# A rotary step on packed rows: transfers collect the rotary rows of five tiles, VectorE turns them in two groups, transfers write them back

## The chip, the cores and the metric

The kernel runs on one core of a Trainium2 chip. The metric is the device time of one execution in microseconds (us). A TensorE, VectorE (DVE), ScalarE (ACT) and GpSimd (POOL) each work through their own list of instructions in order and wait for each other by semaphores; SyncE (SP) only issues transfers (DMAs), also in order. SBUF is the memory on the core with 128 partitions (rows of a tile), PSUM the one that TensorE writes to.

## The reference

One layer of a hybrid decoder, with 1024 tokens of width 1024 in float32. What matters here is the attention half of the token mixer and what stands around it:

```python
h = rmsnorm(x, pre_w_mix[l]) * (1.0 + sc1) + sh1
proj = h @ w_in[l]
aq, ak, av, hq, hf, hi, hg = jnp.split(proj, _SPLITS, axis=-1)
aq = partial_rope(aq.reshape(B, T, ATT_Q_HEADS, ATT_HEAD_DIM))     # 8 heads of 64
ak = partial_rope(ak.reshape(B, T, ATT_KV_HEADS, ATT_HEAD_DIM))    # 2 heads of 64
attn = sliding_window_sink_attention(aq, ak, av, attn_sinks[l])    # window 128
...
def partial_rope(x):                # the first 16 of the 64 numbers of a head
    x1, x2, rest = x[..., :8], x[..., 8:16], x[..., 16:]
    return jnp.concatenate([x1 * cos - x2 * sin, x2 * cos + x1 * sin, rest], axis=-1)
```

So only 16 of the 64 numbers of each head are turned by the rotary step; the other 48 pass. Behind it stand a gated linear recurrence (HGRN2), an output projection and a squared-ReLU MLP, which the change does not touch.

## The kernel before

Matrices are held as a high and a low part, and a product is three matmuls (high by high, high by low, low by high). Tokens are worked on in two halves of 512. The projection is made transposed: a tile `qT{th}_{u}` or `kT{th}` has 128 partitions, which are the 64 numbers of two heads, and 512 columns, which are the tokens of half `th`. There are four q tiles, one k tile and one v tile in each half.

The program is written as one list per engine. A small class `Queue` (lines 26 to 42, its call on line 39 is the line that almost all rows of the profile show) can pin an engine to the order in which the program is written; where an engine is not pinned, a scheduler orders its instructions when the program is built. `DVE.last = marks[...]` puts a piece of VectorE work right behind a marked instruction.

The stretch around the change has these steps.

1. The first half's q, k and v tiles are finished on TensorE. ScalarE copies each from PSUM (`evac`), while TensorE makes k and v of the second half (`pk`, `pv`) and then the second half's q tiles one after the other (`pq`, `q_later`). These q matmuls, and after them the `pv` matmuls with the weights `whv`, are filler: `feed(us)` puts so many of them between the steps of attention.
2. `rope` turns a tile: a VectorE shuffle exchanges rows 0 to 7 with 8 to 15 in each group of 32 partitions, POOL multiplies the shuffled copy by a sine table, VectorE multiplies the tile by a cosine table, and VectorE adds the two. All four run over the full 128 x 512 tile; the tables hold 1 and 0 where nothing is turned. Five tiles of the first half are turned in one go (line 728), before the first scores; the five of the second half one at a time (`rope_late`), between pieces of attention.
3. `attention(tb)` handles a block of 128 tokens in stages: scores `sc` on TensorE (two groups of four heads, `mp` 0 and 1), masked copy to `comb` (VectorE `COPY_PREDICATED`, ScalarE for the block before), maximum `mx` and shifts `nm`, `sd` on VectorE, eight exponentials with sums on ScalarE, `den`, `rd` and the product `comb` on VectorE and POOL, transposes `pT` on TensorE, masked copies `pc` and `pp` on VectorE, values `oT` on TensorE, squares `sqa`, their sum `sqr`, its transpose `ssp`, `ssc`, the root `r_att` on POOL, `dg` on VectorE, the broadcast `rb` on TensorE and the scaling of `aT` on VectorE. The blocks overlap: while block t is between its stages, t+1 and t+2 are in theirs.
4. `split_hv` loads the eight weights `whv` into a pool of three raw buffers (`raw_`), ScalarE copies the high part and VectorE takes the low part; the load into a buffer waits until the low part of the weight three before has been made. `mod_sums` puts one step of a weighted sum over `wada` tiles (`macc`, VectorE) into the stream.

The order on VectorE in step 3 is the program's: an instruction that waits there holds all that stand behind it. The same holds for SP's list of transfers.

Of the kernel before, what the change touches and what calls it, by code (L numbers as in the profile page):

```python
# [47 lines left out]
def hybrid_layer(ctx: ExitStack, tc: tile.TileContext, I, out, dbg=None):  # L48
# [807 lines left out]
    hgw = cload("hgw", [P, 1], pool=tiny1)  # L856
    DVE.last = marks["sqr"]
    lsum = tiny1.tile([P, 4], F32, tag="lsum", bufs=1, name="lsum")
    DVE.tensor_tensor(lsum, le[:, 0, :], le[:, 1, :], ALU.add)
    lrc = tiny1.tile([P, 4], F32, tag="lrc", bufs=1, name="lrc")  # L860
    DVE.reciprocal(lrc, lsum)
    lp = small.tile([P, 2, 4], F32, tag="lp", bufs=1, name="lp")
    DVE.tensor_tensor(lp, le, lrc.unsqueeze(1).broadcast_to([P, 2, 4]), ALU.mult)
    lcs = small.tile([P, 4], F32, tag="lcs", bufs=1, name="lcs")
    DVE.tensor_tensor(lcs, lp[:, 0, :], lp[:, 1, :], ALU.add)
    DVE.last = None
    lb = tiny1.tile([P, 4], F32, tag="lb", name="lb")
    DVE.tensor_tensor(lb, lcs, lp[:, 0, :], ALU.subtract)
    omlb = tiny1.tile([P, 4], F32, tag="omlb", name="omlb")
    DVE.tensor_scalar(omlb, lb, -1.0, 1.0, ALU.mult, ALU.add)  # L870

# [1047 lines left out]
```

## Time and profile before

| | |
|---|---|
| median of 3 runs | 1091.78 us (1091.12 to 1093.92) |
| the profiled execution | 1092.65 us, span 1090.8 us, mean TensorE clock 0.993 |
| TensorE matmul busy in the span | 1068.2 us, 98% |
| VectorE, ScalarE, POOL busy | 818.8, 585.4 and 373.9 us |
| data moved | 206.62 MB |

The busy time of TensorE is that of pipelined matmuls, so 98% says that it is seldom idle, not that it runs at its peak. An idle time of an engine costs something only where the end hangs on it. "Releaser" names the instruction whose semaphore ended a wait.

### The profile page before, as it was taken

Reading aid. Unit: us, or ns where it says so; the run is one execution under the profiler, and the core shown is the slowest. Engines: PE = TensorE matmul, PEld = TensorE weight load, DVE = VectorE, ACT = ScalarE, POOL = GpSimd, SP = SyncE. Lnnn points to the kernel's source line nnn. Section 1 sums busy time; section 2 is a strip of 40 time slices with the busy share of each in tenths; the row PEclk is TensorE's granted clock in tenths of the full one; section 3 lists DMA queues with packets and bytes.
Section 4 is the critical chain, followed back from the end, with each engine's and each line's share of the span. In section 5 each row is a group of like instructions: output and inputs, shape, how many; then the busy total and the mean of one; then the engine's idle time right before and its main releaser. Section 6 shows DMA issues by size and latency. Waiting matters only on the chain.

```text
span 1090.8 us, 15818 instructions
## 1 busy us (share of the span) xinstructions
PE 1068.2 (98%) x5339; PEld 867.1 (79%) x5339; DVE 818.8 (75%) x1345; ACT 585.4 (54%) x1205; POOL 373.9 (34%) x459
## 2 busy tenths in 40 slices
PE   8988999999999999999999999999999999999996
PEld 6766677788888888888888888888888888888885
DVE  4888988878866574559776758776778787899786
ACT  4544544364664764566655555555665544456435
POOL 1253211143234753432543444444333333300014
PEclk9998999999999999999999999999999999999998
DMA  9901300634310252324577776766998888998538
GB/s 355 364 14 43 123 11 1 224 118 134 117 59 28 89 187 93 133 82 144 193 242 250 255 255 224 254 236 238 319 354 305 268 290 273 308 310 276 172 97 139
DMA packets 103264, 206.62 MB, mean 189 GB/s; under 512 B 13200, under 2 KB 13712, under 8 KB 103184
## 3 DMA queue, kind: packets, MB, share of 16 engines
q1 hardware_dynamic: 87696, 158.06, 42.4%
q0 software_dynamic: 15200, 47.20, 14.1%
q8 instruction: 42, 0.69, 0.3%
q10 hardware_dynamic: 288, 0.36, 0.1%
q14 instruction: 38, 0.31, 0.1%
HBM read 150.52 MB, written 55.05 MB: 188 GB/s over the span
## 4 chain that ended last, share of the span: by engine, by line
PE 83%; DVE 7%; ACT 2%; POOL 1%; issue 1%; DVEq 0%; ACTq 0%; POOLq 0%
PE pda L39 16%; PE pua L39 14%; PE pdc L39 8%; PE po L39 8%; PE puc L39 7%; PE phg L39 4%; PE pu L39 4%; PE phq L39 4%; PE pdb L39 4%; PE phf L39 4%; PE pub L39 3%; PE o L39 1%; ACT comb L39 1%; PE pq L39 1%; DVE mx L39 1%; DVE comb L39 1%
## 5 line engine op out<-in xcount | busy, mean ns | idle before, releaser
L39 POOL TENSOR_TENSOR b<-b,b 128x512 f32<-128x512 f32 x64 | 88.1, 1376 | 218.6 <-DMA b<-w_dn 218.2
L39 ACT ACTIVATE dw<-dwr 128x512 fp32r<-128x512 f32 x72 | 45.4, 630 | 50.3 <-DMA dwr<-td 29.0
L39 ACT ACTIVATE s<-s 128x512 f32<-128x512 f32 x84 | 52.9, 631 | 32.2 <-DVE s L39 30.8
L39 DVE TENSOR_TENSOR acc<-pda,acc 128x512 f32<-128x512 f32 x68 | 46.6, 686 | 15.4 <-PE pda L39 14.8
L39 DVE TENSOR_TENSOR dw<-dwr,dw 128x512 fp32r<-128x512 f32 x72 | 51.7, 718 | 8.4 <-ACT dw L39 8.4
L39 POOL DMA_DIRECT2D td<-b x64 | 36.3, 567 | 19.0 <-POOL b L39 19.0
L39 POOL TENSOR_TENSOR rrf<-ssf,mhalf 128x1 f32<-128x1 f32 x7 | 7.7, 1107 | 101.8 <-DVE ssf L39 101.8
L39 ACT ACTIVATE s<-pua 128x512 f32<-128x512 f32 x28 | 16.7, 598 | 43.6 <-PE pua L39 43.3
L39 ACT ACTIVATE comb<-comb,nm 128x128 f32<-128x128 f32 x64 | 24.8, 388 | 26.5 <-DVE sd L39 21.8
L39 DVE TENSOR_TENSOR wt<-s,wt 128x512 fp32r<-128x512 f32 x42 | 35.9, 855 | 2.5 <-ACT wt L39 2.4
L39 ACT ACT_TABLE_LOAD x28 | 35.9, 1283 | 1.7 <-PEq L1912 1.2
L39 DVE SCALAR_TENSOR_TENSOR macc<-wada,cs,macc 128x512 f32<-128x512 f32 x42 | 34.1, 812 | 2.5 <-DMA wada<-wada 1.7
L39 POOL DMA_DIRECT2D b<-w_dn x64 | 34.4, 540 | 2.7 <-issue 2.7
L39 DVE TENSOR_TENSOR wt<-a,wt 128x512 fp32r<-128x512 f32 x42 | 33.9, 806 | 0.9 <-ACT wt L39 0.9
L39 PE MATMUL pua<-bt_0h,wt 128*128 128x512 f32 x84 | 32.7, 389 | 0.0
L39 PE MATMUL pua<-bt_1h,wt 128*128 128x512 f32 x84 | 32.7, 389 | 0.0
L39 PE MATMUL pua<-bt_2h,wt 128*128 128x512 f32 x84 | 32.7, 389 | 0.0
L39 PE MATMUL pua<-bt_3h,wt 128*128 128x512 f32 x84 | 32.7, 389 | 0.0
L39 DVE TENSOR_TENSOR s<-puc,s 128x512 f32<-128x512 f32 x14 | 9.7, 690 | 27.6 <-issue 26.2
L39 DVE TENSOR_TENSOR acc<-pdc,acc 128x512 f32<-128x512 f32 x36 | 24.6, 684 | 7.4 <-PE pdc L39 7.3
L39 PE MATMUL pdc<-dw,du_3h 128*128 128x512 f32 x96 | 29.6, 389 | 0.0
L39 PE MATMUL pda<-dw,du_7h 128*128 128x512 f32 x96 | 29.6, 389 | 0.0
(811 smaller groups left out, 3723.0 us busy)
## 6 DMA issues: line engine op xcount, KB each, us to landing
dur<-ud SPq DMA_DIRECT2D x112, 256.0 KB, 4.5
wada<-wada SPq DMA_DIRECT2D x64, 256.0 KB, 3.6
b<-w_dn POOLq DMA_DIRECT2D x64, 256.0 KB, 5.0
td<-b POOLq DMA_DIRECT2D x64, 256.0 KB, 3.4
dwr<-td SPq DMA_DIRECT2D x64, 256.0 KB, 4.1
a<-w_u SPq DMA_DIRECT2D x56, 256.0 KB, 4.3
dwr<-w_dn SPq DMA_DIRECT2D x48, 256.0 KB, 4.9
ud<-s SPq DMA_DIRECT2D x42, 256.0 KB, 3.3
```

Of the source, the lines that this page charges most:

```text
L39: ins = op(*args, **kw)
```

## The change

The input weights are laid out so that, in each q and k tile, the 16 turned numbers of the upper head are partitions 48 to 63 and those of the lower head partitions 64 to 79, with the two numbers of each pair beside each other. The rotary rows of a tile are then one block of 32 partitions, and the partner of a row is its neighbour.

- `gather` issues three transfers on SP for a tile: its 32 rows into a strip of `R`, and twice 16 rows (every second one) into the strip of `Rr`, so that `Rr` has the rows with neighbours exchanged. A strip starts at partition 0, 32 or 64.
- `rotate` is three VectorE operations for a group: `R` by cosine, `Rr` by sine, and the sum. The groups have 96 partitions (two q tiles and k) and 64 partitions (two q tiles).
- `scatter` writes the strips back into the tiles with one transfer each.

Shuffles and POOL's products are gone. The first half's k tile is copied from PSUM before q tiles 2 and 3, and v last; the transposes of v move one step later. In the second half the group with k waits for q tiles 0 and 1 and stands behind `sd` of block 1, the other one behind `pp` of block 1. The weights `whv` 0 to 2 are loaded by calls ahead of the gathers, the following ones when a buffer is used; SP is pinned to the written order until the last scatter. Six small operations on the decay bounds (`lsum` to `omlb`) move from the end of attention to the place behind the first rotation, the load of `hgw` moves forward, and the `macc` steps are divided: in blocks 2 to 5 one stands behind `sqr` and one behind the scaling of `aT`, where both stood behind `sqr`, and they start one block earlier.

```diff
-    swap = [(i + 8) % 16 if i < 16 else i for i in range(32)]
-
-    def rope(x, th):
-        sh = t_("rope")
-        DVE.stream_shuffle(sh, x, swap)
-        POOL.tensor_tensor(sh, sh, sinT[th], ALU.mult)
-        DVE.tensor_tensor(x, x, cosT[th], ALU.mult)
-        yield
-        DVE.tensor_tensor(x, x, sh, ALU.add)
-        yield
+    def gather(t, R, Rr, j):
+        SP.dma_start(R[32 * j:32 * j + 32, :], t[48:80, :])
+        for b in range(2):
+            SP.dma_start(Rr[32 * j + b:32 * j + 32:2, :], t[49 - b:80:2, :])
+
+    def rotate(R, Rr, n, th):
+        for t, tab in ((R, cosT), (Rr, sinT)):
+            DVE.tensor_tensor(t[:n, :], t[:n, :], tab[th][:n, :], ALU.mult)
+        DVE.tensor_tensor(R[:n, :], R[:n, :], Rr[:n, :], ALU.add)
+
+    def scatter(t, R, j):
+        SP.dma_start(t[48:80, :], R[32 * j:32 * j + 32, :])
...
         spread(tb - 1)
+        if 3 <= tb <= 6:
+            mod_sums(1, "rb")
         yield
...
+    for kb in range(3):
+        load_hv(kb)
+    pin(True, SP)
+    rr = [w_(f"rr{i}", (P, 2, 512)) for i in range(2)]
+    rr = [(t[:, 0], t[:, 1]) for t in rr]
...
         if kb < 6:
-            u = (0, 1, 5, 4, 2, 3)[kb]
-            evac(0, u, pu[u])
+            u = (0, 1, 4, 2, 3, 5)[kb]
+            t = evac(0, u, pu[u])
+            if kb < 5:
+                gather(t, *rr[kb // 3], kb % 3)
...
-    ropes = [rope(x, 0) for x in [ks[0]] + qs[0]]
-    for a, b in zip([None] + ropes, ropes + [None]):
-        if b:
-            next(b)
-        if a:
-            next(a)
+    rotate(*rr[0], 96, 0)
+    rotate(*rr[1], 64, 0)
+    for i, t in enumerate((qs[0][0], qs[0][1], ks[0])):
+        scatter(t, rr[0][0], i)
+    for i in range(2):
+        scatter(qs[0][2 + i], rr[1][0], i)
+    r1 = [m_(f"r1{i}") for i in range(4)]
+    gather(ks[1], r1[0], r1[1], 2)
     pin(False, ACT, DVE, POOL)
...
-    def rope_late(mark):
+    def rope_late(mark, i):
         old, DVE.last = DVE.last, marks[mark]
-        for _ in rope(late.pop(0), 1):
-            pass
+        rotate(r1[2 * i], r1[2 * i + 1], 64 if i else 96, 1)
         DVE.last = old
...
         def done():
-            late.append(evac(1, u, pst()))
+            gather(evac(1, u, pst()), *r1[2 * (u // 2):2 * (u // 2) + 2], u % 2)
...
-    rope_late("sd")
-    rope_late("sd")
     feed(4.0)
     step(1)
     step(1)
-    rope_late("sd")
+    rope_late("sd", 0)
+    scatter_late(0)
...
+        if t == 1:
+            mod_sums(1)
         if 1 < t < 6:
-            mod_sums(2, "sqr")
+            mod_sums(1, "sqr")
...
-        if t < 2:
-            rope_late("pp")
         if t == 0:
+            rope_late("pp", 1)
             split_hv(range(5, 6))
+            scatter_late(1)
+            pin(False, SP)
```

How VectorE's list stands at the first rotation, from the decay bound's `le` on. Before, the first seven of 15 rotary rows:

```order
L39 TENSOR_TENSOR le<-c_lbt,lmx 128x8
L39 STREAM_SHUFFLE rope<-kT_855 128x512
L39 TENSOR_TENSOR kT_855<-kT_855,rope_0_739 128x512
L39 STREAM_SHUFFLE rope<-qT_0_809 128x512
L39 TENSOR_TENSOR qT_0_809<-qT_0_809,rope_0_739 128x512
L39 TENSOR_TENSOR kT_855<-kT_855,rope 128x512
L39 STREAM_SHUFFLE rope<-qT_1_825 128x512
L39 TENSOR_TENSOR qT_1_825<-qT_1_825,rope_0_739 128x512
```

and now, all of it (`rr_816` is the group of two q tiles and k, `rr_817` that of two q tiles):

```order
L39 TENSOR_TENSOR le<-c_lbt,lmx 128x8
L39 TENSOR_TENSOR rr_816<-rr_816,rope_0_741 96x512
L39 TENSOR_TENSOR rr_816<-rr_816,rope_0_745 96x512
L39 TENSOR_TENSOR rr_816<-rr_816 96x512
L39 TENSOR_TENSOR rr_817<-rr_817,rope_0_741 64x512
L39 TENSOR_TENSOR rr_817<-rr_817,rope_0_745 64x512
L39 TENSOR_TENSOR rr_817<-rr_817 64x512
L39 TENSOR_TENSOR lsum<-le 128x4
```

Fifteen operations of 128 partitions became six of 96 or 64, and the six small ones on the decay bounds stand behind them.

SP's list at the same place, which had nothing between the loads `whv2r` and `whv3r` but the load of `hgw`. Here are the first strips, and the end of the first scatter with what stands behind it:

```order
L39 DMA whv2r<-w_hv 128x512
L39 DMA rr_816<-qT_0_819 32x512
L39 DMA rr_816<-qT_0_819 16x512 x2
L39 DMA rr_816<-qT_1_838 32x512
L39 DMA rr_816<-qT_1_838 16x512 x2
L39 DMA rr_816<-kT_856 32x512
L39 DMA rr_816<-kT_856 16x512 x2
L39 DMA rr_817<-qT_2_874 32x512
```

```order
L39 DMA kT_856<-rr_816 32x512
L39 DMA qT_2_874<-rr_817 32x512
L39 DMA qT_3_892<-rr_817 32x512
L39 DMA r_963<-kT_945 32x512
L39 DMA r_964<-kT_945 16x512 x2
L39 DMA r_963<-qT_0_1027 32x512
L39 DMA r_964<-qT_0_1027 16x512 x2
L39 DMA r_963<-qT_1_1090 32x512
L39 DMA r_964<-qT_1_1090 16x512 x2
L39 DMA qT_0_1027<-r_963 32x512
L39 DMA qT_1_1090<-r_963 32x512
L39 DMA kT_945<-r_963 32x512
```

Right behind these stands `whv3r<-w_hv`: the loads of the later weights are now queued behind the write-back of the second half's first group (`r_963`).

VectorE's list behind `sd` of block 1, where the group with the second half's k stands now (before: one shuffle, one product and one sum of `qT_1` at the same places, and six rotary operations on `kT` and `qT_0` behind `sd` of block 0, which are gone):

```order
L39 TENSOR_TENSOR sd_1138<-c_sinks,mx_1134 128x8
L39 TENSOR_TENSOR r_963<-r_963,rope_1_743 96x512
L39 TENSOR_TENSOR r_964<-r_964,rope_1_747 96x512
L39 TENSOR_TENSOR pc_1172<-pT_0_1173,c_fle 128x512
L39 TENSOR_TENSOR r_963<-r_963,r_964 96x512
L39 TENSOR_TENSOR pc_1172<-pT_1_1179,c_fle 128x512
L39 TENSOR_TENSOR den_1151<-sm_1142,es_1140 128x8
```

Two rotary operations stand ahead of the first `pc` and one between the two, where it was one and one. A little further on, the sum `ssc` and the factor `dg` stand later than they did: `ssc` behind two of the masked copies of block 2, and `dg` behind the low part of `whv5`.

```order
L39 TENSOR_TENSOR whv4l<-whv4r,whv4h 128x512
L39 COPY_PREDICATED comb_1257<-c_mle,sc_0_0_1258 128x256
L39 COPY_PREDICATED comb_1257<-c_mle,sc_0_1_1259 128x256
L39 TENSOR_REDUCE ssc_1274<-ssp_1272 128x1
L39 TENSOR_TENSOR whv5l<-whv5r,whv5h 128x512
L39 TENSOR_SCALAR dg_1280<-c_tab,r_att_1278 128x128
```

Before, `ssc` stood ahead of `whv4l`, and `whv5l` behind `dg`.

More of the change, by code (lines that the diff above doesn't have):

```diff
@@ L259, in load_split @@
         hi, lo = mk(name + "h", dt=F32R), mk(name + "l", dt=F32R)
-        for c in range(0, src.shape[1], 512):
+        for c in range(0, 512 if src is None else src.shape[1], 512):
             rw = load_raw(raw_, f"{name}r{c}", src[:, c:c + 512]) if raw is None else raw
@@ L514, in hybrid_layer @@
         if kb == 6:
+            hgw = cload("hgw", [P, 1], pool=tiny1)
             lbt = cload("lbt", [P, 2, 4], pool=tiny1)
@@ L705, in hybrid_layer, with load_hv @@
     att = [attention(tb) for tb in range(TB)]
+    hvr = []
+    def load_hv(kb):
+        hvr.append(load_raw(raw_, f"whv{kb}r", I["w_hv"][kb]))
+    for kb in range(3):
[3 more added lines that the diff above has]
+    rr = [(t[:, 0], t[:, 1]) for t in rr]
     pu1 = [a_ps("pk1")]
@@ L727, in hybrid_layer, with scatter_late @@
     ACT.activation(le, le, AF.Exp)
-    ropes = [rope(x, 0) for x in [ks[0]] + qs[0]]
-    for a, b in zip([None] + ropes, ropes + [None]):
-        if b:
-            next(b)
-        if a:
-            next(a)
-    pin(False, ACT, DVE, POOL)
+    rotate(*rr[0], 96, 0)
[6 more added lines that the diff above has]
+    gather(ks[1], r1[0], r1[1], 2)
+    pin(False, ACT, DVE, POOL)
+    lsum = tiny1.tile([P, 4], F32, tag="lsum", bufs=1, name="lsum")
+    DVE.tensor_tensor(lsum, le[:, 0, :], le[:, 1, :], ALU.add)
+    lrc = tiny1.tile([P, 4], F32, tag="lrc", bufs=1, name="lrc")
+    DVE.reciprocal(lrc, lsum)
+    lp = small.tile([P, 2, 4], F32, tag="lp", bufs=1, name="lp")
+    DVE.tensor_tensor(lp, le, lrc.unsqueeze(1).broadcast_to([P, 2, 4]), ALU.mult)
+    lcs = small.tile([P, 4], F32, tag="lcs", bufs=1, name="lcs")
+    DVE.tensor_tensor(lcs, lp[:, 0, :], lp[:, 1, :], ALU.add)
+    lb = tiny1.tile([P, 4], F32, tag="lb", name="lb")
+    DVE.tensor_tensor(lb, lcs, lp[:, 0, :], ALU.subtract)
+    omlb = tiny1.tile([P, 4], F32, tag="omlb", name="omlb")
+    DVE.tensor_scalar(omlb, lb, -1.0, 1.0, ALU.mult, ALU.add)
     whv = []
     hv = []
-    late = [ks[1]]
-    def rope_late(mark):
+    def rope_late(mark, i):
         old, DVE.last = DVE.last, marks[mark]
-        for _ in rope(late.pop(0), 1):
-            pass
+        rotate(r1[2 * i], r1[2 * i + 1], 64 if i else 96, 1)
         DVE.last = old
+    def scatter_late(i):
+        for j, t in enumerate(qs[1][2:] if i else qs[1][:2] + [ks[1]]):
+            scatter(t, r1[2 * i], j)
     def q_later(u):
@@ L800, in split_hv @@
         for kb in ks:
-            whv.append(load_split(g_, f"whv{kb}", I["w_hv"][kb]))
+            whv.append(load_split(g_, f"whv{kb}", None, raw=hvr[kb]))
+            if kb + 3 < KB:
+                load_hv(kb + 3)
     feed(2.0)
@@ L855, in hybrid_layer @@
     rmask = cload("rmask", [P, 512], pool=Z)
[L856 to L870, printed above, removed]
     am = Z.tile([P, 4, P], F32, tag="am", bufs=1, name="am")
@@ L1873, in layout @@
     perm = [0, 4, 1, 5, 2, 6, 3, 7]
-    A["w_q"] = f(wi[:, :512].reshape(D, 8, 64)[:, perm].reshape(KB, P, 512))
-    A["w_kv"] = f(wi[:, 512:768].reshape(4, 2, P, 256).transpose(0, 2, 1, 3).reshape(4, P, 512))
+    rot = np.arange(16).reshape(2, 8).T.ravel()
+    dims = np.concatenate([np.arange(16, 64), rot, 64 + rot, 64 + np.arange(16, 64)])
+    A["w_q"] = f(wi[:, :512].reshape(D, 8, 64)[:, perm].reshape(D, 4, P)[:, :, dims].reshape(KB, P, 512))
+    wkvp = np.concatenate([wi[:, 512:640][:, dims], wi[:, 640:768]], 1)
+    A["w_kv"] = f(wkvp.reshape(4, 2, P, 256).transpose(0, 2, 1, 3).reshape(4, P, 512))
     A["w_hv"] = f(wi[:, 1792:2304].reshape(KB, P, 512))
@@ L1892, in layout @@
     co, si = np.cos(ang).astype(np.float32), np.sin(ang).astype(np.float32)
-    rope = np.zeros((2, 2, 64, 1024), np.float32)
-    rope[0, :, 16:] = 1.0
-    rope[0, :, :16] = np.concatenate([co, co], 1).T
-    rope[1, :, :16] = np.concatenate([-si, si], 1).T
-    A["rope"] = f(rope.reshape(2, P, 2, 512).transpose(0, 2, 1, 3))
+    rope = np.stack([np.stack([co, co], 2), np.stack([-si, si], 2)]).reshape(2, 2, 512, 16)
+    A["rope"] = f(np.tile(rope.transpose(0, 1, 3, 2), (1, 1, 8, 1)))
     i = np.arange(P)
```

2 lines of the change are left out of this document (1 added, 1 removed).

## The prediction

> **What bounds the kernel now.** First the chain of waits, then the table of stages, then the waits of TensorE in the two stages that the change touches. Shares of the chain by engine (the page):
>
> ```profile
> PE 83%; DVE 7%; ACT 2%; POOL 1%; issue 1%; DVEq 0%; ACTq 0%; POOLq 0%
> ```
>
> Busy times by stage (start and end, length, then PE, PEld, DVE, ACT, POOL; the granted clock):
>
> ```profile
> 75.00:112.00 37.00, 30.58 (x171) 22.29 (x171) 32.59 (x59) 14.98 (x53) 14.58 (x13) 0.86 0.16 47
> 112.00:200.00 88.00, 84.50 (x502) 59.80 (x501) 74.32 (x158) 40.64 (x148) 18.12 (x23) 1.00 0.18 61
> 200.00:380.00 180.00, 179.98 (x1130) 149.65 (x1129) 132.21 (x242) 100.68 (x208) 70.00 (x77) 1.00 0.32 104
> 380.00:1090.00 710.00, 702.23 (x3130) 580.31 (x3128) 527.36 (x779) 388.01 (x719) 250.69 (x321) 1.00 0.69 227
> ```
>
> TensorE is the bound, and its program is nearly the same after the change. So only its idle time and its slow clock can be won. From 75 to 112 it idles 37.00 - 30.58 = 6.42 us, at a clock of 0.86; from 112 to 200, 3.50 us at full clock. From 200 to 380 it idles 0.02 us: what is won before 200 is kept there, since nothing waits for a fixed hour. TensorE's waits from 70 to 112, then from 112 to 200 (total, times, longest):
>
> ```profile
> PE sc L39 <- DVE qT L39: 3.6, 2, 2.6
> PE oT L39 <- ACT comb L39: 2.0, 1, 2.0
> PE pT L39 <- DVE comb L39: 0.7, 1, 0.7
> PE pT L39 <- POOL comb L39: 0.2, 1, 0.2
> ```
>
> ```profile
> PE oT L39 <- DVE pp L39: 2.1, 6, 0.5
> PE rb L39 <- DVE dg L39: 0.7, 1, 0.7
> PE ssp L39 <- DVE sqr L39: 0.5, 1, 0.5
> ```
>
> The largest is the wait of the first scores for the turned tiles. In order of time on TensorE:
>
> ```profile
> 74.80 0.39 PE L39 MATMUL pq<-hlo,wq7h 128*128 128x512 f32 x1
> 76.19 0.49 PE L39 MATMUL sc<-kT,qT 64*128 64x128 f32 x4 [1.00 <-DVE qT L39]
> 79.24 0.80 PE L39 MATMUL sc<-kT,qT 64*128 64x128 f32 x4 [2.56 <-DVE qT L39]
> 79.97 0.79 PE L39 MATMUL pq<-hhi,wq7l 128*128 128x512 f32 x1
> ...
> 84.40 0.47 PE L39 MATMUL pq<-hhi,wq3h 128*128 128x512 f32 x1
> ...
> 101.70 1.98 PE L39 MATMUL oT<-pc,v 128*64 128x512 f32 x4 [2.03 <-ACT comb L39]
> 103.61 0.80 PE L39 MATMUL pq<-hlo,wq1h 128*128 128x512 f32 x1
> 104.20 0.63 PE L39 MATMUL pq<-hhi,wq1l 128*128 128x512 f32 x1
> ...
> 111.59 0.38 PE L39 MATMUL rb<-dg,ones 128*128 128x128 f32 x2
> ```
>
> Each longer wait is paid twice: the matmuls behind it run slowly. Ten start from 79.97 up to 84.40, 0.44 us apart; at the usual 0.23 that is 2.1 us lost, and 0.3 on the scores. Behind the wait of 2.03, `oT` and two matmuls lose some 1.5 (estimates from these durations).
>
> **The change: the first rotation.** VectorE and ScalarE around the rotations:
>
> ```profile
> 68.20 0.73 DVE L39 STREAM_SHUFFLE rope<-kT 128x512 f32<-128x512 f32 x1
> ...
> 93.59 0.68 DVE L39 TENSOR_TENSOR qT<-qT,rope 128x512 f32<-128x512 f32 x1
> 94.19 0.15 DVE L39 TENSOR_TENSOR den<-sm,es 128x8 f32<-128x8 f32 x1
> ...
> 98.31 0.74 DVE L39 STREAM_SHUFFLE rope<-qT 128x512 f32<-128x512 f32 x1
> ...
> 100.88 0.68 DVE L39 TENSOR_TENSOR pc<-pT,c_fle 128x512 f32<-128x512 f32 x1
> ...
> 109.35 0.29 DVE L39 TENSOR_REDUCE ssc<-ssp 128x1 f32<-128x128 f32 x1 [0.69 <-PE ssp L39]
> 109.56 0.68 DVE L39 TENSOR_TENSOR whv4l<-whv4r,whv4h 128x512 fp32r<-128x512 f32 x1
> 110.15 0.77 DVE L39 COPY_PREDICATED comb<-c_mle,sc 128x256 f32<-128x256 int32 x2
> ...
> 110.98 0.29 DVE L39 TENSOR_SCALAR dg<-c_tab,r_att 128x128 f32<-128x128 f32 x1
> ```
>
> ```profile
> 61.05 0.58 ACT L39 ACTIVATE kT<-pq 128x512 f32<-128x512 f32 x1
> ...
> 64.13 0.58 ACT L39 ACTIVATE qT<-pq 128x512 f32<-128x512 f32 x1
> ...
> 91.99 0.57 ACT L39 ACTIVATE qT<-pq 128x512 f32<-128x512 f32 x1
> ```
>
> One product or sum over 512 columns costs VectorE 0.60 us where POOL is quiet (93.59 to 94.19). A group of three is 1.8 us, six are 3.6, in place of 15 operations that began at 68.20 and let the last scores of the first group go at 79.24. The trace has no transfer from SBUF to SBUF. Its nearest rows (KB, us from issue to landing) and SP's issues:
>
> ```profile
> ud<-rl SPq DMA_DIRECT2D x6, 256.0 KB, 2.0
> ...
> w<-postw POOLq DMA_DIRECT2D x2, 256.0 KB, 7.3
> ...
> c_mle<-mle SPq DMA_DIRECT2D x1, 64.0 KB, 2.7
> ...
> c_hmask<-hmask SPq DMA_DIRECT2D x1, 64.0 KB, 2.2
> ```
>
> ```profile
> 45.86 3.70 SPq L39 DMA_DIRECT2D xT<-xT  x8
> ...
> 51.92 0.33 SPq L39 DMA_DIRECT2D c_hgw<-hgw  x1
> 104.67 0.33 SPq L39 DMA_DIRECT2D whv3r<-w_hv  x1
> ```
>
> A transfer costs 0.46 us of SP (3.70 by 8) and lands after L = 2.0 to 7.3 us; I take 2.2, the small table's, because SP's queue is empty from 51.92 to 104.67. The last q tile is copied by 64.71 (one place earlier in the new order), its three transfers are issued by 66.1 and landed by 68.3: the group with k, older by two tiles, doesn't wait at 68.2. It is turned at 70.0, its third write-back is issued at 71.0 and lands at 73.2, before TensorE's arrival at 75.1. So the wait of 3.56 us goes, and 2.4 of slow clock: **6.0 us**. TensorE covers the rotation by the k, v and q matmuls of the second half until 75.1; L could be 4.1 before it shows. The later q tiles' scores come 14 matmuls after that and are free. Everything SP issues more, 40 transfers by 0.46 = 18 us, lies in its empty time. `lsum` to `omlb`, six operations like `den` (0.15 each), lie in VectorE's wait for the scores.
>
> **The second half's first group.** Behind `sd` of block 0 stood six rotary operations, up to 94.19, while the exponentials were done when the copy at 91.99 began: 2.2 us of VectorE's chain go. `den` then comes 6.0 + 2.2 = 8.2 us earlier, so `sd` of block 1 ends at 98.3 - 8.2 = 90.1. The transposes' two short waits (0.9) go on the way. Behind `sd` two rotary operations, `pc`, the sum and `pc` follow: five by 0.6, to 93.1. `oT` starts at 93.2 and not at 101.70: 8.5 us ahead, though TensorE still waits up to 1 us there: it arrives some 7 us (6.0 and 0.9 of waits) before 99.67, the time at which it came before (101.70 less 2.03). What is late next is the transfer: `qT_1` is copied by 86.5 (92.56 less 6.0), its third transfer issued at 87.9, landed at 90.1, and first read at 90.7. L above 2.8 holds VectorE, and `pc`, `den`, the masked copies and `oT` behind it.
>
> **What comes late after it.** From `oT` to `dg` were 110.98 - 101.70 = 9.3 us. Now `ssc` is behind `whv4l` and two masked copies; from 109.56 to 110.85 these are 1.3 us, with the POOL root still to follow. `whv3r` waits on SP for the write-back at 93.1 + 1.4, but its buffer comes free only near 96, so nothing is added. So `dg` is 1.3 later against `oT`, and `rb`, which follows it, is won 8.5 - 1.3 = 7.2, plus 0.3 that `rb` was late against `dg` before: **7.5 us** in all at `rb`. TensorE now waits there, about 2 us.
>
> Whether the clock drops after that wait the trace doesn't say exactly: 0.7 us did not slow it, 2.03 did, 3.56 cost 2.4. Bounds 0 and 2.4; I take **1.0 lost**, since part of a slow stretch is spent ahead of `rb`'s wait and costs nothing there. The Trainium skill (TensorE: Matmul & The Clock Gate, on why this matters for your kernels) says that gaps up to about 3 us between bursts keep the clock up. By that nothing would be lost, and the sum would be 9.9 in place of 8.9. The row at 103.61, slow after 2.03 us, is against it, and I stay with the row.
>
> **Blocks 2 to 7.** Their waits for `pp` and `sqr`, 2.1 + 0.5, come from VectorE's list: two single rotations stood in it, and two `macc` between `sqr` and `ssc`. The first becomes three operations of 0.6, without POOL; the second goes; one `macc` moves to where VectorE waits for the exponentials. The wait of 0.7 at `rb` stays, as `dg` and `rb` both come earlier. I take **2.4** of 3.5; the bounds are 0.8 (only the two blocks with a rotation) and 3.5. Below nothing is excluded while TensorE's own list is unchanged there.
>
> Sum: 7.5 - 1.0 + 2.4 = 8.9 us. The profiled execution took 1092.65, so 1083.75; it lay 0.87 above the median of the runs, which comes to **1083 us**.
>
> **The rivals.**
>
> *Less is kept.* The waits are only moved: `rb` waits 3 us, the clock drops fully (2.4), and blocks 2 to 7 give 0.8: 6.5 - 2.4 + 0.8 = 4.9, 1087 us. For it: VectorE is busy 32.6 of 37 us there. Against: 30 rotary operations of VectorE (three for each of ten tiles) become twelve, and smaller ones.
>
> *More.* All idle time from 75 to 200 and all slow clock go: 6.4 + 3.5 + 3.9 = 13.8, 1078 us. Against: the written order puts `dg` behind `ssc` and two low parts, wherever TensorE is.
>
> *Nothing.* The gain at `oT` is eaten by the low parts of `whv`, whose loads must follow each other through three buffers, and by the later `ssc`: 1090 to 1092 us. For it: `whv4l` and `ssc` follow each other closely now (109.35, 109.56). Against: these loads hang on `whv0l`, which comes earlier with the exponentials.
>
> *Slower: the transfers are late in line.* Each strip is behind others on SP and VectorE waits in order, so a large L is paid at both ends. At the first scores it decides from L = 4.1; at `oT` each us over 2.8 is a us. Around L = 7, as for `w<-postw`, (k is copied third now, 1.5 us before 61.05, and its last strip issued by 61.5) gather, group and write-back end at 61.5 + 7 + 1.8 + 0.9 + 7 = 78.2, nearly where the scores go now, and `oT` loses 4.2: nothing is left. At 8 it is about 1094 us. For it: 40 transfers where there were none. Against: the rows of 2.0 to 2.7, one of them (`ud`) with four times the bytes.
>
> **How the numbers follow.** About 0.3%, 3.3 us, is what a measurement tells from no change. Forecast (gain 6.5 to 12) 0.64, less 0.14, more 0.04: faster 0.82. Nothing 0.10, slower 0.08. The range 1079 to 1089 goes from a gain of 12.8, near all that is there, to one of 2.8, below the smaller gain; about 0.2 is left out, mostly above.
>
> **What would show it.** Right: no wait of `sc` at the first scores, full clock from 75 to 88, a wait of at most about 1 us at the first `oT` and about 2 at `rb` behind it, fewer than 1.5 us of waits for `pp` and `sqr`. Wrong: strips landing after more than 4 us, VectorE idle ahead of a rotation for a DMA, a slow clock after the first `oT` that lasts into block 2, or new waits after 200.

## The result and the profile after

The changed kernel takes **1084.42 us**, median of 6 executions (1083.32 to 1085.08); the kernel before took 1092.64 in its 6 beside them (1091.12 to 1093.92). The ratio is 0.9925, with a 95% interval from 0.9912 to 0.9938. The change wins 8.2 us. The profiled execution took 1084.39 us, with a span of 1082.6.

The table of stages of the changed kernel (start and end, length, then PE, PEld, DVE, ACT, POOL; the granted clock) answers to the one of before:

```profile
75.00:112.00 37.00, 33.60 (x206) 25.01 (x207) 26.61 (x56) 19.37 (x73) 4.66 (x5) 1.00 0.20 58
112.00:200.00 88.00, 86.05 (x506) 62.21 (x505) 73.15 (x145) 37.70 (x131) 15.26 (x22) 1.00 0.29 92
```

TensorE idles 3.40 us from 75 to 112 (6.42 before) and 1.95 from 112 to 200 (3.50 before). The granted clock is 1.00 in the first stage, where it was 0.86. All waits of TensorE in the changed kernel that bear on this (total, times, longest):

```profile
PE rb L39 <- DVE dg L39: 2.9, 2, 2.3
...
PE ssp L39 <- DVE sqr L39: 1.1, 1, 1.1
PE oT L39 <- DVE pc L39: 1.1, 1, 1.1
...
PE pdc L39 <- DVE acc L39: 0.6, 2, 0.3
```

The waits for the turned q tiles, for the exponentials at `oT`, at the transposes and for `pp` are gone. In their place stand 1.1 at the first `oT`, 2.3 at the `rb` behind it and 1.1 for `sqr` of block 6. In order of time on TensorE:

```profile
74.90 0.72 PE L39 MATMUL sc<-kT,qT 64*128 64x128 f32 x8
...
92.92 1.08 PE L39 MATMUL oT<-pc,v 128*64 128x512 f32 x4 [1.08 <-DVE pc L39]
...
103.73 0.49 PE L39 MATMUL rb<-dg,ones 128*128 128x128 f32 x2 [2.32 <-DVE dg L39]
...
417.12 1.91 PE L39 MATMUL x2T<-c_tab,mixn 128*128 128x128 f32 x16
```

and the last of these places in the kernel before:

```profile
426.52 1.91 PE L39 MATMUL x2T<-c_tab,mixn 128*128 128x128 f32 x16
```

Read against the rows of before, the lead grows and shrinks along the way: 8.8 us at `oT` (101.70 to 92.92), 7.9 at `rb` (111.59 to 103.73), 9.4 at the first `x2T`, and 8.2 at the end (spans 1090.8 and 1082.6). What was won at `oT` is partly given back by `rb`. VectorE's rows between the two show where:

```profile
89.68 1.28 DVE L39 TENSOR_TENSOR r<-r,rope 96x512 f32<-96x512 f32 x2
...
92.09 0.68 DVE L39 TENSOR_TENSOR pc<-pT,c_fle 128x512 f32<-128x512 f32 x1
...
98.89 0.69 DVE L39 TENSOR_TENSOR whv3l<-whv3r,whv3h 128x512 fp32r<-128x512 f32 x1 [1.08 <-ACT whv3h L39]
...
101.77 0.28 DVE L39 TENSOR_REDUCE ssc<-ssp 128x1 f32<-128x128 f32 x1
...
103.39 0.29 DVE L39 TENSOR_SCALAR dg<-c_tab,r_att 128x128 f32<-128x128 f32 x1 [0.74 <-POOL r_att L39]
```

VectorE stands in line for `whv3l`, whose load is late, and only then comes to `ssc`; TensorE waits 2.32 us for `dg`. SP issued that load here, when the low part of `whv0` had left its buffer (it ends at 95.6), and not behind a queue of its own transfers, the last of which was issued by 94.1:

```profile
95.66 0.33 SPq L39 DMA_DIRECT2D whv3r<-w_hv  x1
```

The 1.2 us lost between 417 and the end are the two waits for `acc` and their restarts, at 944 and 949; ahead of the second one of VectorE's operations took 1.78 us:

```profile
946.89 1.78 DVE L39 SCALAR_TENSOR_TENSOR gw<-wada,cs,gw 128x512 f32<-128x512 f32 x1
```

In none of the ten other profiles below is there a wait for `acc`, so I take it as a matter of this one execution and not of the change.

### The profile page after: what moved, and what is told of

Its sections match the earlier page's. It is cut to its first block, busy times and chain, and to the rows that moved or that the text cites. A ratio compares the mean times of both kernels' runs of the same rounds, so it can differ in the third digit from the quotient of the medians.

```text
span 1082.6 us, 15845 instructions
## 1 busy us (share of the span) xinstructions
PE 1064.1 (98%) x5339; PEld 864.6 (80%) x5339; DVE 804.9 (74%) x1317; ACT 585.4 (54%) x1205; POOL 357.4 (33%) x449
## 4 chain that ended last, share of the span: by engine, by line
PE 87%; DMA 5%; DVE 5%; ACT 1%; issue 1%; POOL 0%; SPq 0%; DVEq 0%; ACTq 0%
PE pua L39 14%; PE pda L39 14%; PE po L39 8%; PE puc L39 7%; PE pdc L39 7%; PE phg L39 4%; PE pu L39 4%; PE phq L39 4%; PE pv L39 4%; PE pdb L39 4%; PE phf L39 4%; PE pub L39 4%; PE pq L39 2%; DMA wa<-wada 2%; PE o L39 1%; PE oT L39 1%
## 5 line engine op out<-in xcount | busy, mean ns | idle before, releaser
L39 DVE TENSOR_TENSOR dw<-dwr,dw 128x512 fp32r<-128x512 f32 x72 | 54.4, 756 | 9.1 <-ACT dw L39 9.1
L39 POOL TENSOR_TENSOR comb<-comb,rd 128x512 f32<-128x512 f32 x8 | 11.6, 1456 | 70.0 <-ACT hv L39 23.1
```

The source lines that it names most:

```text
L39: ins = op(*args, **kw)
```

## The experiments

Times are medians. The experiments ran in three groups, each on one chip with the kernel before beside it, whose medians were 1092.44 (halves, `macc`, `root_first`), 1092.27 (transfers, `no_rotation`, `reordered`) and 1092.97 (`wait_long`, `reordered_more`).

### Each half of the change alone

`late_in_place` puts the second half back:

```diff
-        rotate(r1[2 * i], r1[2 * i + 1], 64 if i else 96, 1)
+        for _ in rope(late.pop(0), 1):
+            pass
...
-            gather(evac(1, u, pst()), *r1[2 * (u // 2):2 * (u // 2) + 2], u % 2)
+            late.append(evac(1, u, pst()))
```

> The changed kernel with the second half's tiles rotated whole and in place, as before the change: one shuffle (neighbouring rows, as the weights are in the new order), POOL's product and two VectorE operations for each of five tiles, at the old places behind sd and pp; no transfers for them. The first half stays packed. Nothing is left out. Theory (both halves count): the 6.0 us of the first scores stay; den and oT of block 0 come only 6.0 earlier than before the change and not 8.2 to 8.8, so oT starts at about 95.7 and not 92.92; dg again stands ahead of whv5l, so at rb 1.9 of the changed kernel's time is lost; the two blocks with a single rotation wait 0.35 each again; a slow clock behind the wait at oT costs 0 to 1.7. Sum 2.6 to 4.3 slower than the changed kernel: 1087 to 1088.7. Rival (the first scores gave nearly everything, and the second half's transfers only pay for themselves): within 0.7 of the changed kernel, 1084 to 1085.

Measured 1085.88 (1085.06 to 1087.10; ratio to before 0.9946, 0.9934 to 0.9959), 1.5 above the changed kernel and below the 2.6 to 4.3 of the theory, though above the rival. Its rows on TensorE:

```profile
74.35 0.72 PE L39 MATMUL sc<-kT,qT 64*128 64x128 f32 x8
...
94.62 1.08 PE L39 MATMUL oT<-pc,v 128*64 128x512 f32 x4 [2.04 <-ACT comb L39]
...
103.88 0.49 PE L39 MATMUL rb<-dg,ones 128*128 128x128 f32 x2 [0.76 <-DVE dg L39]
...
115.42 0.30 PE L39 MATMUL ssp<-c_tab,sqr 128*128 128x128 f32 x1 [0.29 <-DVE sqr L39]
...
122.63 1.09 PE L39 MATMUL oT<-pp,v 128*64 128x512 f32 x4 [0.54 <-DVE pp L39]
...
128.86 0.30 PE L39 MATMUL ssp<-c_tab,sqr 128*128 128x128 f32 x1 [0.52 <-DVE sqr L39]
```

This execution is 0.55 us ahead from the first scores on (74.35 and 74.90). At `oT` it is then 2.25 us behind the changed kernel (94.62 less 92.92, and 0.55), so the second half's packing wins there what I had reckoned. But at `rb` only 0.70 of it is left (103.88 less 103.73, and 0.55): here `dg` follows `oT` sooner. The rest of the second half's gain, 1.35 us, is the three waits in blocks 1 and 2 that the single rotations cause.

`first_in_place` is the mirror image:

```diff
-    rotate(*rr[0], 96, 0)
-    rotate(*rr[1], 64, 0)
+    ropes = [rope(x, 0) for x in [ks[0]] + qs[0]]
+    for a, b in zip([None] + ropes, ropes + [None]):
+        if b:
+            next(b)
+        if a:
+            next(a)
```

> The mirror image: the first half's five tiles are rotated whole and in place, as before the change, the second half stays packed. Nothing is left out. Theory: the wait of 3.56 us at the first scores and the 2.4 us of slow clock behind it are back, so TensorE comes to oT of block 0 6.0 later; VectorE, freed of six rotary operations behind sd of block 0, is there in time, so the wait of 2.03 us at oT is gone, dg is late by 1.3 against oT, and of this place 1 us is won; blocks 2 to 7 win the 1.6 us they win in the changed kernel; a slow clock behind oT (1.7) may be gone too. Gain against the kernel before 2.5 to 4.3: 1088.3 to 1090. With the other half undone the two gains should add up to the 8.2 of the change within 1.5 us. Rival (the two halves hide each other: VectorE has to be early in both for either to count): under 1 us of gain here, 1091.5 to 1092.6.

Measured 1090.32 (1088.96 to 1090.65, 11 executions; ratio 0.9980, 0.9971 to 0.9989): 2.1 us of gain, 0.3 outside the theory's range and clear of the rival's. The two halves alone give 6.6 and 2.1, together 8.7 against 8.2: they add up within the scatter. Three quarters of the change are the first rotation.

### The divided macc steps

`macc_undone`:

```diff
-        if 3 <= tb <= 6:
-            mod_sums(1, "rb")
...
-        if t == 1:
-            mod_sums(1)
         if 1 < t < 6:
-            mod_sums(1, "sqr")
+            mod_sums(2, "sqr")
```

> The changed kernel with the macc steps as before the change: in blocks 2 to 5 two of them stand together behind sqr, ahead of ssc; none behind the scaling of aT. Nothing is left out. Before the change TensorE waited 2.1 us for pp in six places (0.5 at most) and 0.5 for sqr from block 2 on; in the changed kernel none of the waits for pp is left. Theory (two macc behind sqr hold up ssc, dg and what follows by 0.6 to 0.7 us in a block): four waits for pp of about 0.35 are back, 1.2 to 1.5 us slower, 1085.6 to 1085.9. Rival (the single rotations and POOL's products on VectorE's and POOL's lists made those waits, and macc has room wherever it stands): no wait for pp, 1084.4 within 0.4.

Measured 1084.25 (1082.85 to 1084.62). The time is the rival's: dividing the steps is worth nothing in the sum. Its reason isn't, as it had said that no wait for `pp` would come back. The waits of TensorE from 112 to 195:

```profile
PE oT L39 <- DVE pp L39: 0.9, 3, 0.4
PE rb L39 <- DVE dg L39: 0.5, 1, 0.5
```

Three small waits for `pp` are back, 0.9 us in all and fewer than the 1.2 to 1.5 of the theory, and the wait of 1.1 for `sqr` of block 6, which the changed kernel has, is gone: the division moves the last step of the sum, a split that took 1.53 us there, ahead of that `sqr`. So the division wins at `pp` about what it loses at that `sqr`.

### How much cover the transfers have

`k_late` transfers the first half's k strips four times:

```diff
-                gather(t, *rr[kb // 3], kb % 3)
+                for _ in range(4 if kb == 2 else 1):
+                    gather(t, *rr[kb // 3], kb % 3)
```

> The changed kernel with the three strips of the first half's k tile transferred four times, so that SP issues 5.4 us more (nine issues of 0.6) ahead of the landing that the first rotary group needs; VectorE's and TensorE's order is kept. Nothing is left out. Rows of the changed kernel: the last k strip is issued at 63.7 and the group starts at 67.61, TensorE comes to the first scores at 74.9, landings take 1.8 to 2.2. Theory (the chain strips, rotary group, write-back, scores has a cover of about 3 us and is paid beyond it): last strip issued at 69.1, landed at 71.0, rotated by 72.9, k written back by issue at 74.8 and landed at 76.9; the first scores wait 2.0 us and everything behind comes 2.0 later, with 0 to 1.7 of slow clock, depending on where the wait falls on the grid of 3.41 us: 1086 to 1088. Rival (the cover is larger, for instance because strips land out of SP's order): no wait at the first scores, 1084.4 within 0.4.

Measured 1091.07 (1087.97 to 1092.86, 10 executions): nearly the whole gain is gone. TensorE and SP's queue in its trace:

```profile
80.02 1.23 PE L39 MATMUL sc<-kT,qT 64*128 64x128 f32 x8 [3.62 <-DMA kT<-rr]
```

```profile
58.84 4.46 SPq L39 DMA_DIRECT2D rr<-qT  x6
63.40 9.36 SPq L39 DMA_DIRECT2D rr<-kT  x12
72.80 3.75 SPq L39 DMA_DIRECT2D rr<-qT  x6
76.66 1.16 SPq L39 DMA_DIRECT2D qT<-rr  x2
77.87 0.58 SPq L39 DMA_DIRECT2D kT<-rr  x1
```

The chain is the one I had named, and its size was off: twelve issues to the same rows took 9.36 us, not 7.2, and the write-back of k stands in SP's list behind the gathers of q tiles 2 and 3. This execution starts 1.4 later (first strip at 58.84, in the changed kernel at 57.41), so the k strips end 7.6 later (72.76 less 63.72, and 1.4) and TensorE waits 3.6: the cover is 4.0 us. And a wait of 3.62 cost 6.4 us: from TensorE's arrival at the first scores to `oT` of block 0 it is 24.4 us here (76.40 to 100.80) and 18.0 in the changed kernel (74.90 to 92.92). Behind the wait the clock was at half for two stretches, from 79.22 to 86.05.

`double_late` transfers the strips of the second half's q tile 1 twice, and marks the second rotary product as the place behind which VectorE's next step stands:

```diff
-            gather(evac(1, u, pst()), *r1[2 * (u // 2):2 * (u // 2) + 2], u % 2)
+            t = evac(1, u, pst())
+            for _ in range(2 if u == 1 else 1):
+                gather(t, *r1[2 * (u // 2):2 * (u // 2) + 2], u % 2)
...
+    old, DVE.last = DVE.last, marks["rot"]
     step(0)
+    DVE.last = old
```

> The changed kernel with the three strips of the second half's q tile 1 transferred twice, so that SP issues 1.8 us more ahead of the last landing that the first rotary group of the second half needs; VectorE's order is kept (both products ahead of the first pc, the sum between the two). Nothing is left out. In the trace of the changed kernel the last of these strips was issued by 87.8 and landed 1.9 later, at 89.7, and the group starts at 89.68 without a wait: the cover that I had put at 0.6 us seems used up. Theory (VectorE waits for the strips and holds pc, den, the low parts and dg): the group starts at 91.5, oT of block 0 at 94.7, the wait at rb grows from 2.3 to about 4.0, and the end comes 1.7 later; a wait of over 3.5 us leaves every stretch of 3.41 us half idle wherever the grid lies, so the clock drops in every execution, 0.9 to 1.7 more. 1086.1 to 1087.8. Rival (the transfers are covered, only their issue is near the edge): no DMA wait of VectorE over 0.3, 1084.4 within 0.5.

Measured 1084.65 (1084.50 to 1085.40), within the rival's bounds, but not for the rival's reason:

```profile
89.55 0.69 DVE L39 TENSOR_TENSOR r<-r,rope 96x512 f32<-96x512 f32 x1 [0.20 <-DMA r<-qT]
90.62 0.69 DVE L39 TENSOR_TENSOR r<-r,rope 96x512 f32<-96x512 f32 x1 [0.38 <-DMA r<-qT]
...
92.64 0.17 DVE L39 TENSOR_TENSOR den<-sm,es 128x8 f32<-128x8 f32 x1 [0.74 <-ACT comb L39]
```

```profile
94.23 1.50 PE L39 MATMUL oT<-pc,v 128*64 128x512 f32 x4 [2.80 <-DVE pc L39]
...
104.70 0.49 PE L39 MATMUL rb<-dg,ones 128*128 128x128 f32 x2 [0.39 <-DVE dg L39]
```

VectorE did wait for the strips, 0.58 us: the cover is about 1.2 of the 1.8 us added. `den` and its reciprocal had moved ahead of the second `pc`, against what I said of the order, and made 0.74 more of waiting, so this run doesn't isolate the strips. The wait at `oT` grew by 1.7 and the one at `rb` shrank by 1.9, but a late `oT` wasn't free: counted from the first scores (74.49 here, 74.90 in the changed kernel), `rb` starts 1.4 us later, with the clock at half from 94.75 to 98.16. How much `rb` hangs on `oT` and how much on the low parts of `whv` this run doesn't separate. That the low parts make the wait at `rb` in the changed kernel is shown by `root_first` below.

### What the rotary step still costs

`no_rotation` leaves out all gathers, rotary operations and write-backs.

> The changed kernel without the rotary step: all gathers, rotary operations and write-backs are left out, so queries and keys go into the scores unturned. What the rotary step still costs. Theory (of the step only the order of VectorE's list around the first group of the second half still costs): pc comes 1.2 us earlier and the wait of 1.08 at oT goes; dg is still behind the low parts, which wait for their loads, so most of the 2.3 at rb stays; blocks 1 and 2 have no waits now and win nothing. 1083.0 to 1083.8. Rival 1 (packed and moved off the path, the step costs nothing more): 1084.4 within 0.4. Rival 2 (VectorE's 7 us of rotary work still push everything up to block 2): 1081.5 or less, with the wait at rb under 1 us.

Measured 1082.34 (1081.93 to 1082.49), 2.1 below the changed kernel; the theory's range began at 1083.0. TensorE:

```profile
91.80 1.08 PE L39 MATMUL oT<-pc,v 128*64 128x512 f32 x4
...
102.20 0.49 PE L39 MATMUL rb<-dg,ones 128*128 128x128 f32 x2 [1.54 <-DVE dg L39]
```

The wait at `oT` goes and 1.54 stays at `rb` without any rotary work. The 2.1 us are not the price of the step alone, since VectorE's list came out in another order as well: `ssc` stands ahead of `whv4l` here (99.55 and 100.60), as in the kernel before. Of the 9.9 us between the kernel before (1092.27) and this one the change wins 8.

### Whether a wait slows the clock

Granted clock changes at 77.72, 84.56, 101.62 and 105.04 in the trace before, and next at 1084.66, after the end of TensorE's work: all whole multiples of 3.413 us apart. Cut on that grid, the stretches around the waits read as follows (same columns as the table of stages). Before:

```profile
74.31:77.72 3.41, 1.37 (x8) 0.68 (x7) 3.38 (x6) 0.00 (x0) 2.06 (x2) 1.00 0.00 0
77.72:81.13 3.41, 1.89 (x7) 1.47 (x8) 3.38 (x5) 0.33 (x1) 2.14 (x2) 0.50 0.00 0
...
98.21:101.62 3.41, 1.46 (x7) 0.88 (x5) 3.41 (x8) 3.27 (x18) 1.28 (x1) 1.00 0.00 0
101.62:105.03 3.41, 3.33 (x7) 1.49 (x8) 3.34 (x6) 2.21 (x5) 1.48 (x1) 0.50 0.00 0
```

The changed kernel, whose grid is read off at the end of its trace (1078.44), and `macc_undone`, with a wait of 2.34 at the same `rb`:

```profile
98.83:102.24 3.41, 2.59 (x22) 1.83 (x21) 3.04 (x7) 2.44 (x8) 0.09 (x1) 1.00 0.71 237
102.24:105.65 3.41, 1.92 (x14) 1.78 (x15) 2.67 (x6) 0.95 (x2) 1.03 (x2) 1.00 0.44 122
```

```profile
101.31:104.72 3.41, 1.08 (x9) 1.08 (x10) 2.67 (x8) 1.80 (x5) 1.12 (x2) 1.00 0.61 175
104.72:108.13 3.41, 3.41 (x11) 2.73 (x10) 3.41 (x9) 0.70 (x4) 0.00 (x0) 0.50 0.06 14
```

```profile
103.64 0.49 PE L39 MATMUL rb<-dg,ones 128*128 128x128 f32 x2 [2.34 <-DVE dg L39]
```

The same wait falls into two stretches in the one execution, busy 2.59 and 1.92 of 3.41, and into one in the other, busy 1.08: half clock follows only there. `first_in_place` gives the closest case on the other side, and ahead of it a stretch behind its first scores:

```profile
77.82:81.23 3.41, 2.48 (x8) 1.97 (x9) 3.38 (x5) 0.60 (x1) 2.14 (x3) 0.50 0.00 0
...
108.53:111.94 3.41, 1.67 (x13) 1.58 (x14) 2.66 (x7) 1.21 (x3) 1.13 (x2) 1.00 0.54 138
```

Busy 1.67 kept the clock, busy 1.46 lost it. The same grid laid over all twelve profiles leaves no exception and brings the two sides closer: of the stretches at full clock, one with 1.50 us busy kept it (`k_late`, 109.95 to 113.36), one with 1.48 lost it (`reordered`, 1070.30 to 1073.71, near the end of its work). `late_in_place` has the wait at `oT` of the kernel before again (2.04 us against 2.03), but there it is cut into stretches with 2.55 and 1.83 busy, and the clock stays full. `wait_long` lengthens the wait past what the grid can split:

```diff
+        if not tb:
+            DVE.last = marks["ssc"]
+            for _ in range(3):
+                DVE.last = DVE.tensor_tensor(sq, sq, sq, ALU.mult).ins
         dg = small.tile([P, P], F32, tag="dg", bufs=1, name=f"dg{tb}")
```

> The changed kernel with three added products of 128x512 on VectorE (results not used) between ssc and dg of block 0, so that TensorE's wait at rb grows from 2.3 to about 3.5 us. Nothing is left out. The profiles so far: a stretch of 3.41 us on the grid that held 1.95 us or more of idle TensorE was followed by a slow one (five cases), one with 1.73 or less was not (four cases); the same wait of 2.3 us at rb was followed by half clock in one kernel's profile and by full clock in another's. Theory (the stretch decides, and where the grid lies differs by execution): 3.5 us cannot be cut into two pieces that are both under 1.73, so every execution has a slow stretch behind rb: all mean clocks at 0.996 or 0.997 and none at 0.998 by this place, times in one group instead of two, spread under 1 us; 1.2 to 1.8 later by VectorE and 1.5 by the clock against the quick group of this order (1083.0): 1085.7 to 1086.3. Rival (half clock comes at random, or by the length of a wait that need not be whole): two groups again, one at about 1084.5 with full clock, one 1.5 higher.

Measured 1086.34 (1085.87 to 1087.83), with mean clocks, from the quickest execution to the slowest, of 0.996, 0.996, 0.997, 0.994 and 0.994: no execution at the rival's 1084.5, and none at 0.998. The theory holds in that; the spread is 2.0 and not under 1, since two executions lost more clock than one stretch. That a wait of 3.5 can't be split was a little too strong: with 1.50 us of work enough to keep the clock, two halves of 1.76 would both pass. Its profile:

```profile
104.58 0.49 PE L39 MATMUL rb<-dg,ones 128*128 128x128 f32 x2 [3.52 <-DVE dg L39]
```

```profile
101.75:105.16 3.41, 0.58 (x5) 0.58 (x6) 3.41 (x8) 0.63 (x2) 1.13 (x2) 1.00 0.48 138
105.16:108.57 3.41, 3.41 (x14) 2.93 (x12) 3.22 (x9) 1.10 (x6) 0.00 (x0) 0.50 0.02 5
```

The single executions bear it out. `macc_undone` has two groups: 1082.85 and 1082.99 at mean clocks of 0.997 and 0.998, and 1084.25 to 1084.62 at 0.996. Of 39 executions of the kernel before, 11 at 0.997 average 1091.7 us, 22 at 0.994 or less 1093.0. The mean clock has a part from behind the last matmul in it, so the groups are not clean; that the phase of the grid is the cause of each is argued from the profiles, not seen in every execution.

### A better order of the same work

`root_first` moves two splits behind `dg`:

```diff
-        if t == 0:
-            split_hv(range(3, 5))
-            values_all()
...
+        if t == 0:
+            old, DVE.last = DVE.last, marks["dg"]
+            split_hv(range(3, 5))
+            DVE.last = old
+            values_all()
```

> The changed kernel with one thing moved: in block 0 the splits of whv3 and whv4 stand behind dg on VectorE, so that ssc and dg no longer stand behind two low parts. Nothing is left out. In the trace of the changed kernel ssp is done at 98.9, ssc starts only at 101.77 and dg at 103.39, and TensorE waits 2.32 us at rb (arrival 101.41). Theory (the order of VectorE's list alone makes this wait): ssc at about 98.9, the root on POOL takes the 1.3 us it takes now, dg at 100.5, no wait at rb; oT of block 1 then waits 0.2 at most, so 2.1 us faster, 1082.3 in a run whose clock stays full. Rival (something else is late next: the masked copies, the low parts that the values' matmuls need, or pp of block 1): the wait of 2.3 shows up again within 10 us, under 0.7 us gained, 1083.7 to 1084.4. On the clock: in the trace before, granted clock changes at 77.72, 84.56, 101.62 and 105.04, all on one grid of 3.41 us; the stretch of 3.41 us that ended at 101.62 held 1.95 us of idle TensorE and a slow one followed; in the changed kernel the grid (read off at the end, 1078.44) cuts the wait of 2.32 into 0.83 and 1.49 and no slow one followed. If that is the rule, some executions of the changed kernel lose up to 1.7 us there and others none, and this kernel, with no wait over 1.1 us, never does: its times lie closer together and the median gains up to 0.9 more, 1081.4. If the length of the wait alone decides, the gain is the 2.1 of the wait.

Measured 1084.98 (1084.86 to 1086.33): nothing gained, as the rival said.

```profile
109.91 0.59 PE L39 MATMUL pv<-whv5l,hhi 128*128 128x512 f32 x1 [2.46 <-DVE whv5l L39]
```

The wait at `rb` is gone, and one of 2.46 us stands at `whv5l`, which now came behind the two products of the second half's second rotary group. `reordered` moves that split too, and the first rotary group of the second half behind both `pc`:

```diff
-    rope_late("sd", 0)
-    scatter_late(0)
     feed(2.0)
     step(0)
+    rope_late("pc", 0)
+    scatter_late(0)
...
+            old, DVE.last = DVE.last, marks["dg"]
+            split_hv(range(3, 6))
```

> The changed kernel with three pieces of VectorE's list put in another order, nothing left out: the second half's first rotary group stands behind both pc of block 0 (its results are first read by the scores of block 4), the splits of whv3, whv4 and whv5 stand behind dg. With only the splits of whv3 and whv4 moved the wait of 2.3 us left rb and came back at whv5l (2.46 us), because that split was put behind the rotary group. Theory (these waits are only the order of VectorE's list): oT of block 0 starts at TensorE's arrival, 1.08 us earlier; dg comes before TensorE reaches rb; whv5l ends near 102, ahead of its first use; no wait over 0.7 us is left between 75 and 170 us, and with no stretch of 3.41 us that is half idle the clock never drops. Gain 1.1 + 2.3 = 3.4 us against a run of the changed kernel with full clock (1084.39): 1081.0, and up to 0.9 more at the median. Rival (VectorE is full there: what is taken out of one place is late at the next, as it was with the first reordering): again a wait of 2 us or more at pv, pp or sc, 1083.5 to 1085. The trace that says it: the waits of TensorE from 75 to 130 us.

Measured 1082.16 (1081.94 to 1082.34; ratio to before 0.9907, 0.9893 to 0.9920), 2.3 below the changed kernel, between theory and rival:

```profile
101.10 0.49 PE L39 MATMUL rb<-dg,ones 128*128 128x128 f32 x2 [1.32 <-DVE dg L39]
107.40 1.08 PE L39 MATMUL oT<-pp,v 128*64 128x512 f32 x4 [0.62 <-DVE pp L39]
```

No wait is longer than 1.32, and the four executions lie within 0.4 us, at mean clocks of 0.997 and 0.998. With the rotary step in it this order is as quick as the changed kernel without the step (1082.34). `reordered_more` goes on:

```diff
-        step(t + 2)
+        if t:
+            step(t + 2)
...
+        if t == 0:
+            old, DVE.last = DVE.last, marks["ssc"]
+            step(t + 2)
...
-        if 3 <= tb <= 6:
+        if 3 <= tb <= 5:
             mod_sums(1, "rb")
```

> The reordered kernel (1082.16) with three pieces more put in another order, nothing left out: in block 0 the transpose ssp stands ahead of the first scores of block 2 on TensorE and ssc ahead of their masked copies on VectorE, and the last step of the first modulation row (a split, 1.5 us on VectorE) stands behind dg of block 6 and not ahead of its sqr. In the trace of the reordered kernel VectorE stands idle for 0.91 us ahead of the masked copies and ssc comes at 99.50, though ssp is done at 97.3; TensorE then waits 1.32 at rb, 0.62 and 0.42 for pp of blocks 1 and 2, and 1.15 for sqr of block 6. Theory (each of these waits is the order of the lists): ssc at about 97.3, dg at 98.7, no wait at rb; pp of block 1 comes early enough; the wait for sqr goes. Gain 1.3 + 0.6 + 1.1 = 3.0, less 0.3 for a wait of ssp: 1079.5. Rival (VectorE is full in blocks 0 to 2, what is gained at rb is waited for at pp): only the 1.1 of block 6 is gained, 1081.

Measured **1080.79** (1080.59 to 1081.34; ratio to before 0.9888, 0.9874 to 0.9901), the quickest of all. The gain on the reordered kernel is 1.4 us, where the theory had 2.7 and the rival 1.1:

```profile
108.28 1.08 PE L39 MATMUL oT<-pp,v 128*64 128x512 f32 x4 [1.55 <-DVE pp L39]
```

The waits at `rb` of block 0 and for `sqr` of block 6 are gone, and 1.55 us are waited for `pp` of block 1. From the first scores to these values it is 33.17 us (75.11 to 108.28), against 32.99 in the reordered kernel (74.41 to 107.40): what was gained at `rb` is waited for at `pp`, as the rival said. Between 102 and 108 VectorE has no gap left. Ahead of that it still has two, of 0.98 and 0.50 us, and whether another order can use them wasn't tried.

## Why the prediction was right, point by point

The forecast was 1083 us in a range of 1079 to 1089; it came to 1084.42. Against the profiled execution the sum said 8.9 us of gain, and 8.26 were measured. By its terms:

- **The first rotation, 6.0.** Right. There is no wait at the first scores and the clock stays full; the scores behind them start 6.6 earlier (85.51 before, 78.94 now), of which 0.3 is an earlier arrival. In `late_in_place`, which has this part and not the other, the gain is 6.6.
- **`oT`, 8.5 ahead with a wait of up to 1.** Measured 8.8 ahead, with a wait of 1.08.
- **`dg` 1.3 later against `oT`.** From `oT` to `dg` it is 10.5 us, where it was 9.3. **`rb` won 7.5**: measured 7.9, with a wait of 2.3 where I said about 2. That the write-back on SP adds nothing to the load of `whv3` was right too (issued at 95.66, as the buffer came free). What I left out is that VectorE waits for what is loaded: it stood idle for 1.08 us at `whv3l` (0.53 before) and 0.31 at `whv4l` (none before), ahead of `ssc`. In their place its wait for `ssp` (0.69 before) is gone, so that the 1.3 came out by some luck.
- **1.0 lost to the clock.** Measured 0 in the profiled execution. The bound of about 3 us that the Trainium skill gives (TensorE: Matmul & The Clock Gate, "Why this matters for your kernels") doesn't hold here: waits of 2.03 and 2.34 us were followed by half clock. But the row at 103.61 was no bound either, since the length alone doesn't decide: the same wait of 2.3 us costs 0 or about 1.5, by where it falls on the grid. The reason that I gave for a price between the bounds isn't what decides, so 1.0 was a guess; whether it is near the mean over executions stays open, since their mean clocks don't say how many lost it.
- **Blocks 2 to 7, 2.4.** Mis-sized: from `rb` to `x2T` the lead grows by 1.5 (7.9 to 9.4). Of the waits for `pp` and `sqr` that stood there before, 2.1 and 0.5, the single rotations alone bring back 1.35 (`late_in_place`), the undivided `macc` alone 0.9 (`macc_undone`). The step that failed is that the moved `macc` costs nothing: dividing it makes a wait of its own, 1.1 for `sqr` of block 6, and that takes back what it wins.
- **Nothing after 200.** In the profiled execution 1.2 us were lost at 944 and 949; the ten other profiles have no such wait.

That the sum comes so near is in part luck. The clock that wasn't lost (1.0) and the 0.4 more at `rb` stand against 0.9 less in blocks 2 to 7 and the 1.2 lost at the end. And of the 1.4 us between 1083 and 1084.42, 0.9 come from the last step, which took 0.87 off for a median of three: in six executions the median of the kernel before is 1092.64, where the profiled one lay.

The price of a transfer was right in its landing and wrong in its issue. In the changed kernel (KB, us to landing), and SP's time for six issues:

```profile
rr<-qT SPq DMA_DIRECT2D x8, 32.0 KB, 1.8
qT<-rr SPq DMA_DIRECT2D x4, 64.0 KB, 2.2
```

```profile
63.82 3.70 SPq L39 DMA_DIRECT2D rr<-qT  x6
```

L is 1.8 to 2.2 as taken (2.2), and an issue is 0.6 us, not 0.46. At the first scores the cover was larger than I reckoned (4.0 us on top of the real landing, against 1.9); at the second half's first group it was about 1.2, where I had 0.6.

The rival "slower" had the right mechanism at the right place: `k_late` shows what a late strip does, and a wait of 3.6 us costs 6.4 there. It only needs landings that these transfers don't have.

## What to carry to other kernels

When an in-order engine wins time at one place, follow its list to the next thing another engine waits for: here 1.5 of 2.2 us were given back within 11 us by low-part splits, one of them waiting for a late load, that stood ahead of a small sum; reordering them brought as much as leaving the rotary step out. Move only the work that is read late, and check what slips behind what: the first attempt moved the wait without shortening it. Price a wait of 2 to 3 us on TensorE with and without a slow clock, and look at several executions before taking one profile's clock for the kernel's.

## What the runs showed of the hardware

- The clock is decided on a fixed grid of 3.413 us whose phase differs by execution. In these twelve profiles a stretch at full clock with 1.48 us or less of busy TensorE was followed by half clock, one with 1.50 or more was not. Once slow, a stretch with 0.93 us of idle time did not bring full clock back (`first_in_place`, 77.82 to 81.23), one with 0.08 did (101.62 to 105.03 in the kernel before). The Trainium skill (TensorE: Matmul & The Clock Gate, "What's actually happening") gives such a free-running window of 3413 ns, and the traces agree; that the clock falls only after an idle window they don't bear out, as windows with 1.46 us of work (98.21 in the kernel before) were followed by half clock too.
- A wait of 3.6 us cost 6.4 us in `k_late`, where two stretches ran at half clock.
- VectorE's operation `gw<-wada,cs,gw` over 512 columns takes 0.74 us, but 1.78 at 946.89 of the changed kernel, while GpSimd's product `b<-b,b` ran (946.80 to 948.13). It isn't this execution's alone: 1.67 in the kernel before (946.96, the product from 946.77) and 1.78 in `late_in_place` (946.89, the product from 946.55). That the product holds it up was not tried by moving it.
